# Feed-forward input as seven block products in place of eight, and the conditioning rows as matrix products in four column groups

## The chip, the cores and the metric

One core of one Trainium2 chip runs the whole program. The metric is the device time of one execution in microseconds (us). PE is the matrix engine, PEld its weight loads, DVE the vector engine, ACT the scalar engine, POOL the GpSimd engine, SP the engine whose queue issues the DMA transfers.

## The reference, cut to what matters

Two layers of a diffusion backbone on 640 tokens (128 of context, 512 latent), 1024 features. Each layer is a feed-forward half-step, a token mixing, and a second feed-forward half-step; each begins with an RMS norm and a modulation by rows computed from the condition:

```python
mods = (silu(cond) @ w_ada + b_ada).reshape(..., 9, 1, 1024)   # shift, scale, gate of three sub-layers
h = rmsnorm(x, g) * (1 + scale) + shift
x = x + 0.5 * gate * ((silu(h @ w_in[:, :2816]) * (h @ w_in[:, 2816:])) @ w_out)
```

`w_ada` is 1024 x 9216 for each layer, and there are two conditions, one for the context tokens and one for the latent ones. All is float32.

## The kernel before, in words

Features lie on the 128 partitions, tokens along the free dimension. The state `x` is eight tiles of 128 x 640. Matrix products run in the single-pass float32 type; to keep float32 accuracy each operand is split into a `hi` and a `lo` part, and each product is three passes: hi·hi, hi·lo, lo·hi (`mm3`; the matmul itself is recorded at line 128). For weights, ACT writes `hi` (line 156) and DVE `lo = raw - hi` (line 157) of 128 x 1024 elements at a time, two buffers of each. For activations the helper `split` does the same (lines 167 and 168).

A feed-forward (`ffn`) has 22 steps `pair(i)`: 128 gate columns and 128 up columns over eight contraction tiles, three passes and two halves of the tokens, 96 matmuls of 320 or 322 columns (two columns carry the shift). DVE takes each result out of PSUM and multiplies it by the norm's factor R (line 385), ACT applies SiLU (421), DVE multiplies (423), and `split` makes the operand of the output product. After 8, 15 and 22 pairs (`PARTS`) `out` runs the output product for each of eight tiles of `x`, and `x_update` (366) adds it with three DVE instructions. In the last part, and at the end of the token mixing (`mix`), `Norm.tile` prepares the next sub-layer's operand for each finished tile: squares on ACT (289), their running sum on POOL (291), the scaled `hi` on ACT (300) and `lo` on DVE (301), and the shift columns on POOL (309).

The conditioning rows: `ada_direct` computes three chunks of 512 columns at the start as float32 matmuls with the condition as the 128 x 2 stationary operand; the other 33 chunks are `ada_steps`, four blocks each, in which DVE multiplies a 128 x 1024 block of `w_ada` by the condition and sums it, once for each condition (244). A pump (`RATES`) spreads these blocks over the pairs and outputs of the feed-forwards.

The order of each engine's instructions is fixed when the program is built, by a list scheduler that takes the ready instruction that is earliest in the program by its own cost estimates. On the chip each engine runs its queue in that order, and an instruction waits for its semaphores with everything behind it. PSUM: two double-bank tiles (`PS`), two of one bank (`PH`), two of one bank (`PF`).

Of the kernel before, what the change touches and what calls it, by code (L numbers as in the profile page):

```python
# [25 lines left out]
RATES = (0.8, 0.8, 0.55)  # L26
# [10 lines left out]
PARTS = ((0, 8), (8, 15), (15, 22))  # L37
# [4 lines left out]
# the two halves of the tokens, without and with the columns of the shift  # L42
# [4 lines left out]
# columns of the per-partition vector table  # L47
# [14 lines left out]
class Pump:  # L62
    def __init__(self):
        self.q = []
# [11 lines left out]
def hybrid_step(ctx: ExitStack, tc: tile.TileContext, x_in, cc_in, cb_in, w_ada0, w_ada, pv_in, lam_in, w_fin, w_fout, w_min, w_mout,  # L76
                cache_in, ident_in, rope_in, cnt_in, sel_in,
# [6 lines left out]
    up = ctx.enter_context(tc.tile_pool(name="up", bufs=35))  # L84
# [19 lines left out]
    def E(dt=F32):  # L104
        return tp.tile([128, N], dt, tag="e", name=nm("e"), bufs=5)
# [33 lines left out]
    ident = C([128, 128], name="ident")  # L139
    sel = C([128, 2], name="sel")  # L140
    cnt = C([128, 2, 16], name="cnt")

    def load_raw(src, n):
        raw = wp.tile([128, 1024], F32, tag="raw", name=nm("raw"), bufs=3)
        nc.sync.dma_start(raw[:, :n], src)
        return raw

    def load_w(src, n, eng=None):
        """DRAM [128, n] -> (hi, lo) with hi + lo the weights exactly."""
        raw = load_raw(src, n)  # L150
        return split_w(raw, n, eng)

    def split_w(raw, n, eng=None):
        hi = wp.tile([128, 1024], F32R, tag="hi", name=nm("hi"), bufs=2)
        lo = wp.tile([128, 1024], F32R, tag="lo", name=nm("lo"), bufs=2)
        S.activation(hi[:, :n], raw[:, :n], AF.Copy)  # L156
        (eng or V).tensor_tensor(out=lo[:, :n], in0=raw[:, :n], in1=hi[:, :n], op=ALU.subtract)  # L157
        return hi, lo
# [13 lines left out]
    def lambdas():  # L172
        lv = T()
        nc.sync.dma_start(lv[:, :L * 128], lam_in)
        for l in range(L):
# [11 lines left out]
            lam.append(lm)  # holds -(lambda)  # L187
# [11 lines left out]
    def ada_direct(c, loads):  # L199
        """the products; yields before the row is turned into columns."""  # L200
# [15 lines left out]
    def ada_load(c, k):  # L216
        t = U(F32)
        nc.sync.dma_start(t[:, :512], w_ada0[:, k, c * 512:(c + 1) * 512])
        return t

    def silu_rows():
        """silu of the two conditions, along the free dimension of every partition."""
        r = []
        for i in range(2):
            t = up.tile([128, 1024], F32, tag="P", name=nm("sc"), bufs=3)
# [3 lines left out]
        return r  # L229

    def ada_steps(l, c, spare={}):
        m = []

        def step(b):
            if b == 0:
                m.append(C([128, 4, 2], name="mod"))
            if b in spare:
                raw = spare[b]
                nc.sync.dma_start(raw, w_ada[l, 4 * c + b])
            else:  # L240
                raw = load_raw(w_ada[l, 4 * c + b], 1024)
            dump = sp.tile([128, 1536], F32, tag="KS", name=nm("dump"), bufs=2)
            for i in range(2):
# [1091 lines left out]
```

## Time and profile before

| | |
|---|---|
| median of three runs | 2506.04 us (2505.41 to 2507.21) |
| span of the profiled execution | 2509.4 us |
| PE busy in it | 2446.1 us |
| DVE busy | 1563.7 us |
| ACT busy | 865.5 us |
| POOL busy | 304.9 us |

The profile gives the profiled execution's span and no separate time for it; the span is 3.4 us above the median of the runs. Busy times are sums of instruction durations; matmuls are pipelined, so the distance from one start to the next says more of PE than a duration.

### The profile page before, as it was taken

Reading aid. Unit: us, or ns where it says so; the run is one execution under the profiler, and the core shown is the slowest. Engines: PE = TensorE matmul, PEld = TensorE weight load, DVE = VectorE, ACT = ScalarE, POOL = GpSimd, SP = SyncE. Lnnn points to the kernel's source line nnn. Section 1 sums busy time; section 2 is a strip of 40 time slices with the busy share of each in tenths; the row PEclk is TensorE's granted clock in tenths of the full one; section 3 lists DMA queues with packets and bytes.
Section 4 is the critical chain, followed back from the end, with each engine's and each line's share of the span. In section 5 each row is a group of like instructions: output and inputs, shape, how many; then the busy total and the mean of one; then the engine's idle time right before and its main releaser. Section 6 shows DMA issues by size and latency. Waiting matters only on the chain. (4 is left out here: it accounts for less than half of the span.)

```text
span 2509.4 us, 39961 instructions
## 1 busy us (share of the span) xinstructions
PE 2446.1 (97%) x16529; PEld 2405.3 (96%) x16529; DVE 1563.7 (62%) x2550; ACT 865.5 (34%) x1417; POOL 304.9 (12%) x329
## 2 busy tenths in 40 slices
PE   8999999998998999999999999999999999999998
PEld 4999999998898999999999999999989999999998
DVE  5766766668886666666666556556788664334335
ACT  3222212356664221212332122224666442122223
POOL 3000000143224000000110000003513230000002
PEclk8999999999999999999999999999999999999999
DMA  7444444224322444444333333332242122222224
GB/s 261 154 142 136 132 138 138 90 89 137 117 66 89 137 135 135 133 137 135 101 110 110 120 115 116 115 102 89 90 143 85 53 74 70 75 76 70 82 72 130
DMA packets 91317, 282.10 MB, mean 112 GB/s; under 512 B 9600, under 2 KB 17664, under 8 KB 91136
## 3 DMA queue, kind: packets, MB, share of 16 engines
q1 hardware_dynamic: 91136, 279.56, 34.6%
q8 instruction: 130, 2.13, 0.3%
q14 instruction: 51, 0.42, 0.1%
HBM read 264.58 MB, written 14.94 MB: 111 GB/s over the span
## 5 line engine op out<-in xcount | busy, mean ns | idle before, releaser
L128 PE MATMUL S<-u,hi 128*128 128x320 f32 (+1 forms) x9056 | 1720.7, 311 | 14.8 <-DVE x L366 7.3
L128 PEld LDWEIGHTS S<-u,hi 128*128 128x128 f32 x9056 | 1434.7, 189 | 18.8 <-ACT hi L156 7.7
L128 PE MATMUL S<-u,lo 128*128 128x320 f32 (+2 forms) x4528 | 1047.6, 310 | 4.4 <-DVE lo L157 4.4
L128 PEld LDWEIGHTS S<-u,lo 128*128 128x128 f32 x4528 | 765.2, 189 | 5.4 <-DVE lo L157 5.4
L156 ACT ACTIVATE hi<-raw 128x1024 fp32r<-128x1024 f32 (+2 forms) x336 | 345.2, 1027 | 1117.7 <-PE S L128 649.9
L244 DVE SCALAR_TENSOR_TENSOR dump<-raw,sc 128x1024 f32<-128x1024 f32 x262 | 322.9, 1234 | 175.9 <-DMA raw<-in_w_ada_dram 172.7
L157 DVE TENSOR_TENSOR lo<-raw,hi 128x1024 fp32r<-128x1024 f32 (+1 forms) x296 | 351.3, 1187 | 10.7 <-ACT hi L156 8.0
L385 DVE TENSOR_TENSOR t<-S,R 128x642 f32<-128x642 f32 x176 | 145.2, 825 | 331.8 <-PE S L128 325.2
L128 PE MATMUL F<-u,hi 128*128 128x320 f32 (+1 forms) x1056 | 236.9, 316 | 3.9 <-DVE t L547 3.3
L366 DVE SCALAR_TENSOR_TENSOR x<-S,gate,x 128x128 f32<-128x128 f32 (+2 forms) x264 | 99.8, 433 | 184.8 <-PE S L128 184.6
L128 PEld LDWEIGHTS F<-u,hi 128*128 128x128 f32 x1056 | 175.1, 190 | 5.5 <-DVE t L547 3.8
L128 PE MATMUL F<-u,lo 128*128 128x320 f32 (+1 forms) x528 | 155.2, 313 | 0.0
L167 ACT ACTIVATE u<-t 128x640 fp32r<-128x640 f32 x88 | 65.1, 740 | 208.4 <-DVE t L423 208.4
L157 POOL TENSOR_TENSOR lo<-raw,hi 128x1024 fp32r<-128x1024 f32 (+1 forms) x40 | 89.4, 2234 | 258.3 <-ACT hi L156 212.2
L168 DVE TENSOR_TENSOR u<-t,u 128x640 fp32r<-128x640 f32 x88 | 72.6, 825 | 62.1 <-ACT u L167 62.1
L421 ACT ACTIVATE t<-t 128x128 f32<-128x128 f32 (+1 forms) x176 | 89.6, 556 | 57.2 <-DVE t L385 55.1
L301 DVE SCALAR_TENSOR_TENSOR u<-x,scl,u 128x128 fp32r<-128x128 f32 x96 | 94.3, 996 | 7.9 <-ACT u L300 6.9
L128 PEld LDWEIGHTS F<-u,lo 128*128 128x128 f32 x528 | 97.6, 190 | 0.0
L291 POOL TENSOR_TENSOR t<-t,t 128x640 f32<-128x640 f32 x42 | 73.5, 1749 | 161.6 <-ACT t L289 161.4
L568 POOL MEMSET pl<- 128x8 f32 x4 | 0.4, 107 | 761.2 <-DVE dump L244 761.1
L423 DVE SCALAR_TENSOR_TENSOR t<-t,t 128x128 f32<-128x128 f32 (+1 forms) x176 | 88.7, 545 | 0.0
L716 DVE TENSOR_REDUCE s<-S 128x1 f32<-128x640 f32 x96 | 77.4, 814 | 2.7 <-PE S L128 2.4
(184 smaller groups left out, 1382.6 us busy)
## 6 DMA issues: line engine op xcount, KB each, us to landing
raw<-in_w_fin_dram SPq DMA_DIRECT2D x176, 512.0 KB
raw<-in_w_ada_dram SPq DMA_DIRECT2D x131, 512.0 KB
raw<-in_w_fout_dram SPq DMA_DIRECT2D x72, 448.0 KB
raw<-in_w_min_dram SPq DMA_DIRECT2D x36, 512.0 KB
raw<-in_w_fout_dram SPq DMA_DIRECT2D x32, 512.0 KB
u<-in_w_ada_dram SPq DMA_DIRECT2D x24, 256.0 KB
KS<-kd SPq DMA_DIRECT2D x16, 384.0 KB
raw<-in_w_mout_dram SPq DMA_DIRECT2D x16, 384.0 KB
```

Of the source, the lines that this page charges most:

```text
L128: PE.matmul(out, lhsT, rhs, start=start, stop=stop)
L156: S.activation(hi[:, :n], raw[:, :n], AF.Copy)
L157: (eng or V).tensor_tensor(out=lo[:, :n], in0=raw[:, :n], in1=hi[:, :n], op=ALU.subtract)
L168: V.tensor_tensor(out=dst_lo, in0=src, in1=dst_hi, op=ALU.subtract)
L244: V.scalar_tensor_tensor(out=dump[:, :D], in0=raw, scalar=1.0, in1=rows[i], op0=ALU.mult, op1=ALU.mult, accum_out=m[0][:, b, i:i + 1])
L291: G.tensor_tensor(out=sq[:, :N], in0=sq[:, :N], in1=self.acc[:, :N], op=ALU.add)
L301: (eng or V).scalar_tensor_tensor(out=lo[:, a:b], in0=x[d][:, a:b], scalar=s, in1=hi[:, a:b], op0=ALU.mult, op1=ALU.subtract)
L366: V.scalar_tensor_tensor(out=xs, in0=ps[h][:, a:b], scalar=g[:, d % 4, c:c + 1], in1=xs, op0=ALU.mult, op1=ALU.add)
L385: V.tensor_tensor(out=t[:, :TX], in0=whole(ps), in1=norm.R, op=ALU.mult)
L421: S.activation(g[:, a:b], g[:, a:b], AF.Silu, bias=g[:, N + c:N + c + 1])
L423: V.scalar_tensor_tensor(out=u[:, a:b], in0=u[:, a:b], scalar=u[:, N + c:N + c + 1], in1=g[:, a:b], op0=ALU.add, op1=ALU.mult)
L716: V.tensor_reduce(out=m, in_=s[:, :, :HN], axis=AX.XY, op=ALU.max, negate=True)
```

## The change

`w_fin`'s pair is a 2 x 2 block matrix: gate and up columns by the first and the last four contraction tiles. The operand is a 2 x 2 block matrix as well: first and last four contraction tiles by two halves of the tokens. The changed `pair` forms their product with seven block products in place of eight, a Winograd form of Strassen's scheme: DVE adds blocks of weights (`s3`, `a21`, `s2`, `s4`), each of the seven weight blocks is split into hi and lo, and the seven products of 12 matmuls of 322 columns accumulate in two PSUM regions `A` and `D` that are read in between, and a third, `B`. The operand's seven forms are made by `FastNorm`, in place of `Norm`, once for each feed-forward: four sums on DVE and seven splits for each of four k. The first two pairs of the program stay plain (`NPLAIN`) while those forms are made. The parts of the output product are five in place of three, its tiles go in `ORDER`, and `x_update_joined` uses two DVE instructions in place of three. Weights are split 512 columns at a time, four buffers of each kind.

`ada_steps` goes: `ada_rounds` computes two chunks of 512 columns at a time in four steps. Each step loads two 128 x 1024 blocks of `w_ada` and issues four float32 matmuls, with a 128 x 32 stationary operand that holds the condition in two columns, each to its own 32 partitions of one PSUM bank. After the fourth step ACT copies the bank, and four small float32 matmuls with the 128 x 4 constant `groups` turn rows to columns and add the groups that belong together. A third buffer set (`P`) holds the blocks; `ada_direct` computes chunk 1 too. `E` tiles move to the pool of `U` tiles, 38 of them in place of 35.

```diff
-RATES = (0.8, 0.8, 0.55)
+RATES = (0.29, 0.29, 0.2)
-PARTS = ((0, 8), (8, 15), (15, 22))
+PARTS = ((0, 5), (5, 10), (10, 14), (14, 18), (18, 22))
...
+HLB = 4
+NPLAIN = 2
+ORDER = (0, 4, 1, 5, 2, 6, 3, 7)
+HW = N // 2 + 2
...
+    class Weights:
+
+
+        def __init__(self, raw, n, eng=None):
+            self.parts = [self.piece(raw[:, c:min(c + 512, n)], eng) for c in range(0, n, 512)]
+
+        @staticmethod
+        def piece(src, eng=None):
+            n = src.shape[-1]
+            hi = wp.tile([128, 512], F32R, tag="hi", name=nm("hi"), bufs=HLB)
+            lo = wp.tile([128, 512], F32R, tag="lo", name=nm("lo"), bufs=HLB)
+            S.activation(hi[:, :n], src, AF.Copy)
+            (eng or V).tensor_tensor(out=lo[:, :n], in0=src, in1=hi[:, :n], op=ALU.subtract)
+            return hi, lo
...
-    def silu_rows():
-            nc.sync.dma_start(t, cb_in[:, i * D:(i + 1) * D])
-            S.activation(t, t, AF.Silu)
-            r.append(t)
...
-    def ada_steps(l, c, spare={}):
...
-        def step(b):
...
-                raw = load_raw(w_ada[l, 4 * c + b], 1024)
-            dump = sp.tile([128, 1536], F32, tag="KS", name=nm("dump"), bufs=2)
-            for i in range(2):
-                V.scalar_tensor_tensor(out=dump[:, :D], in0=raw, scalar=1.0, in1=rows[i], op0=ALU.mult, op1=ALU.mult,
-                                       accum_out=m[0][:, b, i:i + 1])
-            if b == 3:
-                V.tensor_tensor(out=m[0], in0=m[0], in1=bada(l, c), op=ALU.add)
-                mods[l][c] = m[0]
...
+    def ada_rounds(l, c):
+
+
+        ps = []
+
+        def step(r):
+            if r == 0:
+                ps.append(PH())
+            for k in (2 * r, 2 * r + 1):
+                w = up.tile([128, 1024], F32, tag="P", name=nm("wa"), bufs=3)
+                nc.sync.dma_start(w, w_ada[l, k, :, c * 512:(c + 2) * 512])
+                for h in range(2):
+                    q = 32 * (2 * (k % 2) + h)
+                    PE.matmul(ps[0][q:q + 32, :], sc32[:, k, :], w[:, h * 512:(h + 1) * 512], start=r == 0, stop=r == 3)
+            if r == 3:
+                row = T()
+                S.activation(row[:, :512], ps[0], AF.Copy)
+                pt = PH()
+                for b in range(4):
+                    mm(pt[:, 4 * b:4 * b + 4], row[:, b * 128:(b + 1) * 128], groups, True, True)
+                for h in range(2):
+                    m = C([128, 4, 2], name="mod")
+                    V.tensor_tensor(out=m, in0=pt[:, 0:16].rearrange("p (b h c) -> p b h c", b=4, h=2)[:, :, h, :], in1=bada(l, c + h), op=ALU.add)
+                    mods[l][c + h] = m
+
+        return [lambda r=r: step(r) for r in range(4)]
...
+    class FastNorm:
...
+        def staged(self, d):
+            t = T()
...
+            for c, h, a, b in ((0, 0, 0, NC), (1, 0, NC, HN), (1, 1, HN, N)):
+                S.activation(t[:, a + 2 * h:b + 2 * h], x[d][:, a:b], AF.Copy, scale=self.scale(d, c))
+            G.tensor_copy(self.view(t)[:, :, HN:HW], self.shift_tile(d // 4)[:, d % 4])
+            return t
...
+        def sums(self, k, b1, b2, late=False):
+            B11, B12, B21, B22 = b1[:, :HW], b1[:, HW:], b2[:, :HW], b2[:, HW:]
+            n, m = T(), T()
+            N1, T3, N2, T4 = n[:, :HW], n[:, HW:], m[:, :HW], m[:, HW:]
+
+            def form(name, src):
+                u = self.view(U())
+                split(u[:, 0], u[:, 1], src)
+                self.f[name, k] = u
+
+            if not late:
+                form("B11", B11)
+                form("B21", B21)
+            V.tensor_tensor(out=T3, in0=B22, in1=B12, op=ALU.subtract)
+            V.scalar_tensor_tensor(out=N2, in0=T3, scalar=-1.0, in1=B11, op0=ALU.mult, op1=ALU.subtract)
+            form("N2", N2)
+            form("T3", T3)
+            V.tensor_tensor(out=N1, in0=B11, in1=B12, op=ALU.subtract)
+            form("N1", N1)
+            V.scalar_tensor_tensor(out=T4, in0=N2, scalar=-1.0, in1=B21, op0=ALU.mult, op1=ALU.subtract)
+            form("T4", T4)
+            if not late:
+                form("B22", B22)
...
+        def tile(self, d):
+
+            self.squares(d)
+            self.st[d] = self.staged(d)
+            if d >= 4:
+                self.sums(d - 4, self.st.pop(d - 4), self.st.pop(d))
...
+    def product(ps, piece, act, start):
+
+        hi, lo = piece
+        for k in range(4):
...
-        def pair(i):
...
+        def pair(i, first):
+
+
+            rg, ru = load_raw(wi[i, 0], 1024), load_raw(wi[i, 1], 1024)
+            a11, a12, a21, a22 = rg[:, :512], rg[:, 512:], ru[:, :512], ru[:, 512:]
+            s2, s3, s4 = FT([128, 512]), FT([128, 512]), FT([128, 512])
+            piece = Weights.piece
+
+            def add(o, a, b):
+                V.tensor_tensor(out=o, in0=a, in1=b, op=ALU.add)
+
+            p = PS()
+            A, D, B = p[:, 0, :HW], p[:, 1, :HW], PF()[:, :HW]
+            g, u = T(), T()
+            w = piece(a11)
+            product(A, w, norm.get("B11"), True)
+            S.activation(g[:, :HW], A, AF.Copy)
+            w = piece(a12)
+            add(s3, a11, a21)
+            add(a21, a21, a22)
+            add(s2, a21, a11)
+            product(B, w, norm.get("B21"), True)
+            if first:
+                norm.stats_sum()
+            V.tensor_tensor(out=g[:, :HW], in0=B, in1=g[:, :HW], op=ALU.add)
+            w = piece(s2)
+            product(A, w, norm.get("N2"), False)
+            S.activation(u[:, :HW], A, AF.Copy)
+            w = piece(s3)
+            add(s4, s2, a12)
+            product(D, w, norm.get("T3"), True)
+            S.activation(u[:, HW:], D, AF.Copy)
+            if first:
+                norm.stats_spread()
+            w = piece(a21)
+            product(A, w, norm.get("N1"), False)
+            V.tensor_tensor(out=u[:, HW:], in0=A, in1=u[:, HW:], op=ALU.add)
+            w = piece(a22)
+            product(D, w, norm.get("T4"), False)
+            V.tensor_tensor(out=u[:, :HW], in0=D, in1=u[:, :HW], op=ALU.add)
+            w = piece(s4)
+            product(A, w, norm.get("B22"), False)
+            V.tensor_tensor(out=g[:, HW:], in0=A, in1=norm.R[:, HW:], op=ALU.mult)
+            V.tensor_tensor(out=g[:, :HW], in0=g[:, :HW], in1=norm.R[:, :HW], op=ALU.mult)
+            V.tensor_tensor(out=u, in0=u, in1=norm.R, op=ALU.mult)
+            activation(i, g, u, HN)
...
-            hi, lo = load_w(wo[d, :, k0 * 128:k1 * 128], (k1 - k0) * 128)
-            mm3([ps[:, 0], ps[:, 1]], CN, hi, lo, acts[k0:k1], range(k1 - k0))
-            x_update(d, ps=[ps[:, 0], ps[:, 1]], gate=gate)
+            w = load_w(wo[d, :, k0 * 128:k1 * 128], (k1 - k0) * 128)
+            mm3(joined(ps), CN, w, acts[k0:k1], range(k1 - k0))
+            x_update_joined(d, ps, gate)
...
         gate = None
         for k0, k1 in PARTS:
             for i in range(k0, k1):
-                pair(i)
+                if l == 0 and sub == 0 and i < NPLAIN:
+                    plain_pair(i)
+                    if i == 0:
+                        for k in range(4):
+                            norm.late(k)
+                else:
+                    pair(i, i == 0)
+            while gate is None and mods[l][2 * (3 * sub + 2) + 1] is None:
+                pump.step()
...
-                for d in range(KT):
+                for d in ORDER:
                     out(k0, k1, d, gate, nx)
         return nx
...
```

## Rows read from the trace of the kernel before

**Rows 1.** The page's first part: busy us, share of the span, instructions.
```profile
PE 2446.1 (97%) x16529; PEld 2405.3 (96%) x16529; DVE 1563.7 (62%) x2550; ACT 865.5 (34%) x1417; POOL 304.9 (12%) x329
```

**Rows 2.** Stages: window, length, busy of PE, PEld, DVE, ACT, POOL; clock, DMA, GB/s.
```profile
200.00:494.00 294.00, 294.00 (x2000) 294.00 (x2000) 191.00 (x296) 75.95 (x101) 9.88 (x18) 1.00 0.40 128
2040.00:2440.00 400.00, 400.00 (x2717) 400.00 (x2715) 156.55 (x210) 98.21 (x124) 0.00 (x0) 1.00 0.23 74
```

**Rows 3.** Whom PE waited for, longest first: us, times, longest.
```profile
PE S L731 <- ACT e L722: 14.8, 12, 2.7
PE S L128 <- DVE x L366: 7.3, 6, 1.7
```

**Rows 4.** Timeline of DVE over one pair: start, us, what.
```profile
1310.65 0.82 DVE L385 TENSOR_TENSOR t<-S,R 128x642 f32<-128x642 f32 x1
1311.39 1.21 DVE L157 TENSOR_TENSOR lo<-raw,hi 128x1024 fp32r<-128x1024 f32 x1
...
1324.92 0.82 DVE L385 TENSOR_TENSOR t<-S,R 128x642 f32<-128x642 f32 x1
```

**Rows 5.** Groups of instructions with shapes apart: busy us, mean ns, idle before.
```profile
L244 DVE SCALAR_TENSOR_TENSOR dump<-raw,sc 128x1024 f32<-128x1024 f32 x262 | 322.9, 1234 | 175.9 <-DMA raw<-in_w_ada_dram 172.7
L157 DVE TENSOR_TENSOR lo<-raw,hi 128x1024 fp32r<-128x1024 f32 x224 | 273.1, 1219 | 9.8 <-ACT hi L156 8.0
L168 DVE TENSOR_TENSOR p<-S,p 128x512 fp32r<-128x512 f32 x64 | 43.8, 685 | 8.8 <-ACT p L167 8.4
L547 DVE TENSOR_TENSOR t<-F,R 128x322 f32<-128x322 f32 x24 | 11.7, 488 | 9.4 <-PE F L128 9.3
L168 DVE TENSOR_TENSOR u<-t,u 128x640 fp32r<-128x640 f32 x88 | 72.6, 825 | 62.1 <-ACT u L167 62.1
L423 DVE SCALAR_TENSOR_TENSOR t<-t,t 128x512 f32<-128x512 f32 x88 | 65.6, 745 | 0.0
L167 ACT ACTIVATE p<-S 128x512 fp32r<-128x512 f32 x64 | 38.2, 597 | 26.9 <-DVE p L168 17.0 <-PE H L128 4.8 <-PE S L731 4.2
L421 ACT ACTIVATE t<-t 128x512 f32<-128x512 f32 x88 | 62.4, 709 | 0.0
```

**Rows 6.** Timeline of PE at the start: float32 matmuls, then the first shift.
```profile
37.41 7.03 PE L128 MATMUL F<-u,silu_c 128*2 128x512 f32 x16
45.18 0.41 PE L211 MATMUL H<-ident,t 2*128 2x2 f32 x4 [0.74 <-ACT t L207]
45.52 1.28 PE L128 MATMUL H<-ones,t 128*128 128x1 f32 x10
...
50.60 0.64 PE L128 MATMUL S<-u,hi 128*128 128x322 f32 x1 [3.02 <-POOL u L309]
```

**Rows 7.** Timeline of PE in an output product.
```profile
160.27 0.45 PE L128 MATMUL S<-u,lo 128*128 128x320 f32 x2
160.56 0.75 PE L128 MATMUL S<-u,hi 128*128 128x320 f32 x4
161.15 0.45 PE L128 MATMUL S<-u,lo 128*128 128x320 f32 x2
```

**Rows 8.** Timeline of DVE at the end of a token mixing.
```profile
785.10 1.12 DVE L366 SCALAR_TENSOR_TENSOR x<-S,mod,x 128x128 f32<-128x128 f32 x3
786.15 1.26 DVE L301 SCALAR_TENSOR_TENSOR u<-x,scl,u 128x512 fp32r<-128x512 f32 x2
787.33 0.66 DVE L366 SCALAR_TENSOR_TENSOR x<-S,mod,x 128x128 f32<-128x128 f32 x2
787.91 1.59 DVE L301 SCALAR_TENSOR_TENSOR u<-x,scl,u 128x512 fp32r<-128x512 f32 x1
789.43 0.54 DVE L366 SCALAR_TENSOR_TENSOR x<-S,mod,x 128x320 f32<-128x320 f32 x1
789.89 0.33 DVE L301 SCALAR_TENSOR_TENSOR u<-x,scl,u 128x128 fp32r<-128x128 f32 x1
790.15 1.12 DVE L366 SCALAR_TENSOR_TENSOR x<-S,mod,x 128x128 f32<-128x128 f32 x3
```

More of the change, by code (lines that the diff above doesn't have):

```diff
@@ L380, in tick, with activation @@
                 credit[0] -= 1.0
-        def pair(i):
-            def evac(ps):
+        def activation(i, g, u, cb):
+            lb = HW + HN
+            for a, b, c in ((0, NC, cb), (NC, lb, lb)):
+                S.activation(g[:, a:b], g[:, a:b], AF.Silu, bias=g[:, c:c + 1])
+            for a, b, c in ((0, NC, cb), (NC, lb, lb)):
+                V.scalar_tensor_tensor(out=u[:, a:b], in0=u[:, a:b], scalar=u[:, c:c + 1], in1=g[:, a:b],
+                                       op0=ALU.add, op1=ALU.mult)
+            hi, lo = U(), U()
+            split(*[t[:, :N].rearrange("p (h n) -> p h n", h=2) for t in (hi, lo)], FastNorm.view(u)[:, :, :HN])
+            acts[i] = (hi, lo)
+            tick(2.0)
@@ L384, in evac, with plain_pair, half @@
+        def plain_pair(i):
+            def half(ps, w, h):
+                n = (HN, HW)[h]
+                for k in range(KT):
+                    w0, w1 = w.at(k)
+                    a = norm.f[norm.blocks(k)[h], k % 4]
+                    ah, al = a[:, 0, :n], a[:, 1, :n]
+                    for p, (w_, a_) in enumerate(((w0, ah), (w0, al), (w1, ah))):
+                        mm(ps[:, :n], w_, a_, k == 0 and p == 0, k == KT - 1 and p == 2)
+            def evac(p, sign):
                 t = T()
-                V.tensor_tensor(out=t[:, :TX], in0=whole(ps), in1=norm.R, op=ALU.mult)
@@ L386, in evac @@
-                return t
-            first = w_first if l == 0 and sub == 0 and i == 0 else None
-            hi, lo = first[0] if first else load_w(wi[i, 0], 1024)
-            p = PS()
-            pg = halves(p)
-            if first:
-                hi2, lo2 = first[1]
-                p2 = PS()
-                pu = halves(p2)
-                mm3(pg, CX, hi, lo, norm.xp, hs=(0,))
-                mm3(pu, CX, hi2, lo2, norm.xp, hs=(0,))
+                for h, n in enumerate((HN, HW)):
+                    V.scalar_tensor_tensor(out=t[:, h * HW:h * HW + n], in0=p[:, h, :n], scalar=sign, in1=norm.R[:, h * HW:h * HW + n],
+                                           op0=ALU.mult, op1=ALU.mult)
@@ L797, in mix @@
         rq8 = [None, None]
-        kxs = [sp.tile([128, 2, 128], F32R, tag="kc", name=nm("kx"), bufs=3) for _ in range(2)]
+        kxs = [FT([128, 2, 128], F32R, "kx") for _ in range(2)]
         gvcx = vctx_tiles()
@@ L1139, in mix @@
         ends = mix_ends()
-        for d in range(KT):
+        for i, d in enumerate(ORDER):
             if d in opened:
@@ L1187, in hybrid_step @@
     lds[0] = [ada_load(0, k) for k in range(KT)]
-    rows = silu_rows()
-    for f in ada_steps(0, 1, {3: cache_tile()}):
-        f()
-    c0 = ada_direct(0, lds[0])
+    lds[1] = [ada_load(1, k) for k in range(KT)]
+    c0, c1 = ada_direct(0, lds[0]), ada_direct(1, lds[1])
     def first_shift():
         next(c0), next(c0), next(c0, None)
+        next(c1), next(c1), next(c1, None)
         for d in SHO:
@@ L1199, in hybrid_step @@
     nc.sync.dma_start(cnt, cnt_in)
+    nc.sync.dma_start(groups, groups_in)
     pump = Pump()
@@ L1247, in _tables @@
     sel[64:, 1] = 1.0
-    return dict(ident=np.eye(128, dtype=np.float32), rope=rope, cnt=cnt, sel=sel)
+    groups = np.zeros((128, 4), np.float32)
+    for q in range(4):
+        for c in range(2):
+            groups[32 * q + c, 2 * (q % 2) + c] = 1.0
+    return dict(ident=np.eye(128, dtype=np.float32), rope=rope, cnt=cnt, sel=sel, groups=groups)
 def _layout(i):
```

243 lines of the change are left out of this document (150 added, 93 removed).

## The prediction

> **What bounds the kernel now.** I read the shares of the whole page first: PE is busy 97% of the span, DVE 62% [rows 1]. Shares are averages, so I then took stages. In two long stretches of feed-forward PE is busy for every microsecond, with the clock at its upper level, while DVE is free for 35% and 61% of the time [rows 2]. The list of whom PE waited for says the same: its longest entries, 14.8 us for the softmax of the token mixing and 7.3 us for the state update, are small beside 2509.4 us [rows 3]. So a feed-forward costs what PE's matmuls cost, and the reader should expect the change to be decided by PE's sum: what leaves PE against what comes to it.
>
> One pair is 14.27 us from one evacuation to the same one of the next pair [rows 4]; over 96 matmuls that is 0.1486 us each. In the output product six matmuls of 320 columns take 0.88 us from start to start, 0.147 us each [rows 7].
>
> **What leaves PE.** 86 of the 88 pairs go from 96 matmuls to 84: 86 x 12 x 0.1486 = 153.4 us. Such a pair is then 84 x 0.1486 = 12.5 us. The token mixing and the output products keep their matmuls.
>
> **What comes to PE.** The conditioning blocks leave DVE: 262 instructions, 322.9 us [rows 5]. DVE bounded nothing in those stages, so their absence gives back nothing by itself. They come back as 16 calls of `ada_rounds`, 64 steps of four float32 matmuls with 512 columns. The nearest row is `ada_direct`, whose eight matmuls of 512 columns appear as 16 instructions in 7.03 us, so each float32 matmul is two instructions of 0.44 us [rows 6]. The stationary operand there has 2 columns and here 32, and all outputs there begin at partition 0. No row shows matmuls in different column groups side by side. The bounds for a step are therefore eight instructions in a row, 3.52 us, and four groups side by side, 2 x 0.44 = 0.88 us; for 64 steps 225 us and 56 us. I take a value between: the two instructions of a matmul stand next to each other in the queue and need the same columns. If PE starts instructions in queue order, the second of group 0 waits for the first, and the first of group 1 can start only beside it. Each following group adds one slot: five slots for four groups, 2.2 us, and 64 x 2.2 = 141 us.
>
> By the Trainium skill, page "TensorE: Matmul & The Clock Gate", section "Part 3: Packing small matmuls", matmuls on different tiles overlap but begin and end strictly in program order; no run here shows it yet. By that rule the sum is the one I take.
>
> The turn of rows to columns: 16 calls x 4 float32 matmuls, two instructions each, by the ten of the norm's sum in 1.28 us [rows 6]: 128 x 0.128 = 16 us. At the start `ada_direct` for chunk 1 adds 16 x 0.44 + 0.4 = 7.4 us, of which the 3.0 us that PE waited for the shift's copies can be covered [rows 6]; I take 4, bounds 0 and 7.4.
>
> **What DVE gets.** Per pair: seven `lo` and four sums of 512 columns (0.685 us), five instructions of 322 columns (0.488), one of 644 and one `lo` of 640 (0.825 each), two multiplications (1.09 together) [rows 5]. Sum of durations: 7.5 + 2.4 + 1.65 + 1.1 = 12.7 us. Neighbours in the queue overlap by 0.08 us (a 0.82 us instruction is followed after 0.74) [rows 4]; for 20 instructions that leaves 11.1 us. PE has 12.5. So DVE is at 90% or just over the top, and the cost lies between nothing and, with 12.7 plus 0.5 us of waiting for ACT's halves, 0.7 us a pair, 60 us in all. Buffers for four pieces let splits run three products ahead, 5.4 us, against 0.6 + 0.69 us to make one, so I take 0.2 us a pair: 17 us. If that cover goes, PE stands behind each `lo` for about 1.3 us, in program order with everything queued. ACT gets seven halves (0.597) and three copies (about 0.45): with the SiLU (two, about 1.1) and the split (0.74) some 7.4 us a pair, under PE's time [rows 5].
>
> **Where stages meet.** `FastNorm` makes seven splits and four sums for two tiles of the state, 11 instructions of 322 columns: 5.5 x 0.41 to 0.49 = 2.3 to 2.7 us of DVE a tile. Now two tiles take 5.05 us at the end of the mixing, 2.3 of it state update, so 1.4 us a tile is the present preparation [rows 8]. New time a tile: 2.5 - 1.4 + 2.5 = 3.6, where PE's twelve matmuls take 1.8. That is 9 us over eight tiles, at the ends of two mixings. In the last part of the middle feed-forward, PE has 24 x 0.147 = 3.5 us a tile and DVE 1.0 + 0.6 + 2.5 = 4.1: 5 us. With a microsecond each for the last forms, 26 us, bounds 10 and 40. The first forms of the program are hidden behind the two plain pairs (28.5 us).
>
> Five parts in place of three put the chain from the last product through SiLU to the split, some 6 us, at eight more places; what hides it is the other PSUM tile's output product, up to 2 x 3 x 0.88 = 5.3 us for parts of four pairs. I take 5 us, bounds 0 and 20. Against these gaps, the conditioning matmuls depend on nothing near them and can fill some: -8 us of the 22. Their loads are as many as before but no longer share the weights' buffers; DVE waited 172.7 us for them in 131 blocks [rows 5], and PE would stand 1.3 us a load if three buffers were not enough, but they are asked for a step ahead, which is over 20 us at the pump's new rate. That `E` moves to the pool of `U` I cost at nothing: 38 tiles in place of 40 hold what a mixing has open; 10 us if they don't.
>
> **The sum**, on the profiled span: 2509.4 - 153.4 + 141 + 16 + 4 + 17 + 26 + 5 - 8 = 2557. The median of the runs is 3.4 below the span: 2553.6, slower by 1.9%.
>
> **The rivals.**
>
> *All four groups side by side* (faster). Then a step is 0.88 us, 85 us less in all: 2469 us. For it: the matmuls of a step are independent, write different partitions, and stand together. Against it: the order of the pairs of instructions above. It decides from a step of 1.46 us on: without the 141 us the sum is 2416, and (2509.4 - 2416) / 64 = 1.46. The Trainium skill, page "TensorEngine Tiling (Array Packing)", section "Theoretical Speedup", gives up to four times for dimensions of at most 32; by it the time would be this rival's. No row here bears it out or excludes it.
>
> *No overlap at all* (slower still). A step is 3.52 us: 84 us more, 2638. For it: every float32 matmul of the trace follows the one before by its full 0.44 us [rows 6], though all of those are in the same columns.
>
> *DVE as the bound of the pairs.* Durations as they stand make 12.7 us against PE's 12.5, and an order fixed by estimates leaves holes on an engine that is nearly full. At 0.9 us lost a pair in place of 0.2 it gives 60 us more: 2614.
>
> **How the numbers follow.** Chances: five slots a step 0.40; side by side 0.32; no overlap 0.18; DVE as the bound 0.10. The likeliest gives 2554, its own range 2525 to 2590 by the bounds of the small terms. The range over the cases reaches from 2452, below the side-by-side case with its small terms at their lower ends, to 2628; left out are most of the no-overlap case above it (about 0.12) and 0.05 below. What a measurement of this kernel can tell from no change is about 0.2%, 5 us. Faster: the side-by-side case and a little of the likeliest with its terms low, 0.33. Same: 0.06, where a step comes near 1.46 us. Slower: 0.61.
>
> **What would show it.** In the changed profile: a pair of 84 matmuls should be 12.5 to 12.9 us long; a step of eight float32 instructions should start over about 1.8 us and end after 2.2, each group's first instruction beside the second of the group before. Starts a few nanoseconds apart and 0.9 us in all would mean the first rival; 0.44 us between all of them the second. DVE over 95% busy in the pairs, with PE waiting for `lo`, would mean the third. At the end of the mixings the waits of PE for the state update should grow from 7 to about 25 us. The prediction is wrong above all if a step costs under 1.46 us, or if pairs take 13 us or more.

## The result, and the profile after

The changed kernel takes 2733.95 us (median of 4 runs, 2733.24 to 2738.06) against 2506.62 for the kernel before: ratio 1.091, 95% interval 1.0895 to 1.0926. I had forecast 2554, at most 2628. The direction came out as forecast, the size did not: 180 us are missing in my sum. The direction was luck: with the 89 us that the conditioning is measured at below, in place of my 149, my own sum would have said 2494, faster.

The page of the changed kernel, its line of busy times (they count overlapping instructions once, so they are not sums of durations; the line of before is in [rows 1]):

```profile
PE 2542.1 (93%) x16157; PEld 2320.0 (85%) x16157; DVE 1843.4 (67%) x3450; ACT 1231.4 (45%) x2460; POOL 301.0 (11%) x375
```

PE has 372 instructions fewer, and its share of the span went down, not up: it stands. The list of whom PE waited for (total us, times, longest) names the place; the entries of before are in [rows 3]:

```profile
PE S L497 <- ACT t L620: 45.5, 49, 1.2
PE S L497 <- ACT hi L169: 21.0, 34, 0.6
PE S L134 <- DVE x L511: 18.0, 6, 4.5
PE H L134 <- DMA u<-qd: 11.2, 3, 8.5
...
PE H L258 <- DMA wa<-in_w_ada_dram: 4.6, 8, 1.4
```

The two longest entries are matmuls of `product` (L497) that waited for ACT, for the copy of the sum A (L620) and for the `hi` of a piece (L169). Together they are 66.5 us, less than the 158 that they turn out to cost: the list counts from the recorded end of the matmul before, and it leaves out 35 of the 86 pairs, where conditioning matmuls stand where the other 49 have the first of the two waits. A pair in the last feed-forward, where no conditioning runs, from one multiplication by R to the next on DVE (start, duration; before [rows 4]):

```profile
2353.14 0.82 DVE L637 TENSOR_TENSOR t<-t,R 128x644 f32<-128x644 f32 x1
...
2368.07 0.82 DVE L637 TENSOR_TENSOR t<-t,R 128x644 f32<-128x644 f32 x1
```

So 14.93 us, where I had 12.5 to 12.9 and the kernel before 14.27. Within that pair PE's timeline (start, duration; in brackets the idle time and what ended it) shows where it stands:

```profile
2357.82 0.31 PE L497 MATMUL S<-u,lo 128*128 128x322 f32 x1
2359.09 0.57 PE L497 MATMUL S<-u,hi 128*128 128x322 f32 x2 [0.96 <-ACT t L620]
...
2360.83 0.31 PE L497 MATMUL S<-u,lo 128*128 128x322 f32 x1
2361.77 0.90 PE L497 MATMUL S<-u,hi 128*128 128x322 f32 x4 [0.62 <-ACT hi L169]
```

From start to start these two places take 1.27 and 0.94 us where neighbours take 0.15: 1.12 and 0.79 us lost, and five of 0.1 beside them; the matmuls themselves are as fast as before. ACT at the same time:

```profile
2358.08 0.63 ACT L169 ACTIVATE hi<-f 128x512 fp32r<-128x512 f32 x1 [0.20 <-PE S L497]
2358.61 0.42 ACT L620 ACTIVATE t<-S 128x322 f32<-128x322 f32 x1
...
2361.09 0.63 ACT L169 ACTIVATE hi<-raw 128x512 fp32r<-128x512 f32 x1 [0.81 <-PE S L497]
2361.62 0.42 ACT L624 ACTIVATE t<-S 128x322 f32<-128x322 f32 x1
```

Read the rows together. Products are named by their operand's form (N2, T3 and so on). The last matmul of N2 that reads its `hi` ends at 2357.98, and N2, into A, at 2358.13. ACT makes a `hi` that had waited for the buffer which N2 held, then copies A, and at 2359.09, with the copy done, the product T3 begins. But T3 writes D, the other bank. In the built program its first matmul waits for just the count that the copy L620 reaches; N1, into A, waits for the copy of D (L624); T4, into D, for DVE's reading of A (L629); and B22, into A, for DVE's reading of D (L632). Each waits for one reading more than its own bank needs. A and D are `p[:, 0]` and `p[:, 1]` of one tile.

The second place is less direct. The matmuls at 2361.77 and 2362.02 are not N1's: they belong to the next pair's first product and stand ahead of N1 in PE's queue. They wait for their `hi`, which had waited for the buffer that T3 held. N1 begins behind them at 2362.17, just after the copy of D has ended (2362.04).

The conditioning is another matter than I thought. A step whose eight instructions stand together, and a split one (six):

```profile
74.54 1.07 PE L258 MATMUL H<-wa,sc 128*32 128x512 f32 x8
75.54 0.42 PE L497 MATMUL F<-u,hi 128*128 128x322 f32 x1
...
133.58 1.06 PE L258 MATMUL H<-wa,sc 128*32 128x512 f32 x6
```

The groups do run side by side: in the trace the first instructions of the four matmuls start 7 ns apart and the second ones, again 7 ns apart, 0.45 us later. But only 22 steps stand together; most are split into three matmuls and one, and each piece costs about 1 us. Counted from the starts of PE's instructions around each insertion, the 64 steps take 119 us, 1.86 each.

### The profile page after: what moved, and what is told of

It reads as the page before. It is cut to its first block, busy times and chain, and to the rows that moved or that the text cites. A ratio compares the mean times of both kernels' runs of the same rounds, so it can differ in the third digit from the quotient of the medians.

```text
span 2731.3 us, 42282 instructions
## 1 busy us (share of the span) xinstructions
PE 2542.1 (93%) x16157; PEld 2320.0 (85%) x16157; DVE 1843.4 (67%) x3450; ACT 1231.4 (45%) x2460; POOL 301.0 (11%) x375
## 5 line engine op out<-in xcount | busy, mean ns | idle before, releaser
L497 PE MATMUL S<-u,hi 128*128 128x322 f32 x4128 | 964.6, 322 | 70.7 <-ACT t L620 45.5
L497 PEld LDWEIGHTS S<-u,hi 128*128 128x128 f32 x4128 | 685.3, 189 | 193.9 <-ACT t L620 89.1
L169 ACT ACTIVATE hi<-raw 128x512 fp32r<-128x512 f32 (+2 forms) x696 | 414.1, 596 | 868.9 <-PE S L497 384.5
L134 PE MATMUL S<-u,hi 128*128 128x320 f32 (+3 forms) x3552 | 698.4, 315 | 35.9 <-DVE x L511 18.0
L497 PE MATMUL S<-u,lo 128*128 128x322 f32 x2064 | 629.2, 310 | 0.0
L134 PEld LDWEIGHTS S<-u,hi 128*128 128x128 f32 x3552 | 567.7, 191 | 61.4 <-ACT hi L169 18.6
L170 DVE TENSOR_TENSOR lo<-raw,hi 128x512 fp32r<-128x512 f32 x616 | 398.9, 649 | 181.4 <-ACT hi L169 173.9
L134 PE MATMUL S<-u,lo 128*128 128x320 f32 (+3 forms) x1776 | 421.2, 312 | 2.6 <-DVE lo L170 2.6
L497 PEld LDWEIGHTS S<-u,lo 128*128 128x128 f32 x2064 | 392.1, 191 | 0.8 <-issue 0.8
L169 ACT ACTIVATE hi<-f 128x512 fp32r<-128x512 f32 x258 | 162.3, 631 | 250.9 <-PE S L497 174.0
L170 DVE TENSOR_TENSOR lo<-f,hi 128x512 fp32r<-128x512 f32 x258 | 177.3, 687 | 38.6 <-ACT hi L169 33.0
L497 PE MATMUL F<-u,hi 128*128 128x322 f32 x688 | 157.4, 314 | 0.9 <-ACT hi L169 0.7
L629 DVE TENSOR_TENSOR t<-S,t 128x322 f32<-128x322 f32 x86 | 42.4, 493 | 154.3 <-PE S L497 154.3
```

Source lines behind the costliest of these rows:

```text
L134: PE.matmul(out, lhsT, rhs, start=start, stop=stop)
L169: S.activation(hi[:, :n], src, AF.Copy)
L170: (eng or V).tensor_tensor(out=lo[:, :n], in0=src, in1=hi[:, :n], op=ALU.subtract)
L497: PE.matmul(ps, w_, a, start=start and k == 0 and p == 0, stop=k == 3 and p == 2, skip_group_check=True)
L629: V.tensor_tensor(out=u[:, HW:], in0=A, in1=u[:, HW:], op=ALU.add)
```

## Experiments

**Theories.** *One tile*: a product waits for the evacuation of the product before it, since the two sums share a tile; remove that, and the pair is 12.5 to 13 us. *Ring*: the four buffers of `hi` and `lo` are too few, and PE stands behind pieces ("if that cover goes", in my prediction). DVE as the bound, my third rival, falls by the rows already: it is busy for 298.41 of 441 us in the last feed-forward (the row stands under e1).

**e1, A and D in tiles of their own.**

```diff
-            p = PS()
-            A, D, B = p[:, 0, :HW], p[:, 1, :HW], PF()[:, :HW]
+            A, B, D = PS()[:, 0, :HW], PF()[:, :HW], PF()[:, :HW]
```

> Edit: the sums A and D of a pair, two banks of one PSUM tile in the changed kernel, get a tile each (D takes the second buffer of the F pool); nothing else. One-tile theory: a product into one bank waits for the evacuation of the other, because both are one tile. In the changed kernel's steady pair (14.93 us) the matmuls alone take 84 x 0.149 = 12.5; the two long stalls are 1.12 and 0.79 us. Without the waits a pair should be 12.5 to 13.0 us, so 86 x 2.0 to 2.4 = 170 to 210 us go; in the order of the instructions 53 of the conditioning steps now stand with all four matmuls together, against 22, about 1 us less each, another 20 to 35. Together 2490 to 2545 us. Ring theory: PE waits because the four buffers of hi and lo let a piece be made only when the product four before it is done; the ring is unchanged here, so pairs stay above 14 us and the time above 2650.

2575.53 us, 158 less. The pair of e1 on DVE, and then the last feed-forward in windows of after (first row) and of e1 (second): busy us of PE, PEld, DVE, ACT, POOL with their counts, granted clock, DMA.

```profile
2344.92 0.82 DVE L636 TENSOR_TENSOR t<-t,R 128x644 f32<-128x644 f32 x1
...
2357.56 0.82 DVE L636 TENSOR_TENSOR t<-t,R 128x644 f32<-128x644 f32 x1
```

```profile
2244.00:2685.00 441.00, 407.57 (x2619) 387.88 (x2617) 298.41 (x527) 175.21 (x319) 0.00 (x0) 1.00 0.22 71
```

```profile
2135.00:2530.00 395.00, 394.69 (x2644) 391.76 (x2643) 303.03 (x537) 176.52 (x324) 0.00 (x0) 1.00 0.25 81
```

The pair is 12.64 us here, 12.62 in most, and PE idles for 0.3 of 395 us. The one-tile theory stands. The time is 30 us above the range I gave it, so the rest lies outside the pairs. e1 changes more than the waits: the scheduler now puts 53 steps together in place of 22, and counted as above the 64 steps take 87 us in place of 119. In the last feed-forward, which has no steps, e1 gains 49 us; in the first three 36, 32 and 42.

**e2 and e3, a fifth buffer of hi and lo**, with A and D in one tile (e2) and in two (e3).

```diff
-HLB = 4
+HLB = 5
...
-        t = up.tile([128, 1024], F32R, tag="P", name=nm("p"), bufs=3)
+        t = up.tile([128, 1024], F32R, tag="P", name=nm("p"), bufs=2)
```

> Edit: on the changed kernel, five buffers of hi and lo in place of four (paid for with two in place of three of the tiles of 1024 columns that the conditioning loads and the mixing share); A and D stay one tile. One-tile theory: the waits for the evacuations stay, but a copy no longer stands behind a hi that waits for a buffer (0.63 us): the stall behind N2 goes from 1.12 to about 0.5, the one behind T3 from 0.79 to about 0.4, so 1.0 us a pair and 86 us in all: about 2645, 2600 to 2690. Ring theory: nearly all of the 2.4 us a pair goes: 2520 to 2560.

> Both edits: A and D in tiles of their own, and five buffers of hi and lo. One-tile theory: no more than 20 us under the run with the tiles of their own alone, or the same. If the ring is a second, independent stall of a pair, another 0.3 to 0.6 us a pair go, 25 to 50 us.

e2: 2701.62, e3: 2589.05. In e2 the steady pair falls by the 1.0 us expected (most are 13.9 us; the last feed-forward 423 us in place of 442), but the buffers given up cost 14 and 9.5 us in the mixings, and the total misses my range by 12 us. In e3 the pair is the same 12.6 us as in e1; the time is 13.5 us longer, 7 and 11 of it in the mixings. The ring delays the copy that PE waits for; once PE no longer waits for that copy, it costs the pairs nothing.

**e4, all conditioning matmuls in one column group** (on e1; both chunks of a call are now summed into one row, so the modulation is another one).

```diff
-                    q = 32 * (2 * (k % 2) + h)
-                    PE.matmul(ps[0][q:q + 32, :], ...
+                    PE.matmul(ps[0][0:32, :], ...
...
```

> Edit: on the kernel with A and D in tiles of their own, all conditioning matmuls write the first column group, so that both chunks of a call are summed into one row and the modulation is another one; the number of matmuls and their shapes stay. In the changed kernel a step whose eight instructions stand together takes 1.08 us of PE's queue (first instructions 7 ns apart, the second ones 0.45 us later). Theory of overlapping groups: in one group each of the eight takes about 0.45 us by itself, a step 3.5 us, so 64 x 2.4 = 155 us more than with four groups. Rival, that the instructions would overlap in one group as well: the same time within 10 us.

2727.8 in its one run, 152 more than e1. The step there:

```profile
76.64 3.62 PE L257 MATMUL H<-wa,sc 128*32 128x512 f32 x8
```

3.62 us against 1.07: the four groups are what makes them overlap. For 64 steps that would be 163 us.

**e5, all pairs as eight products**, the rest as changed.

```diff
-                if l == 0 and sub == 0 and i < NPLAIN:
-                    plain_pair(i)
...
-                else:
-                    pair(i, i == 0)
+                plain_pair(i, i == 0)
```

> Edit: the changed kernel with all 88 pairs as eight products (the kernel's own plain pair), and with the operands that these need; five parts, buffers and conditioning matmuls stay. It prices everything of the change but the seven products. With tiles of their own the seven products' pair is 12.62 us against 14.27, so 142 us are given back here. Terms as measured there: 2509 before, 87 to 119 for the conditioning matmuls, 15 for the turn of rows, and the rest of what the run with own tiles lost (about 100 us in all between its 2573 and 2509 - 142 + 87 + 15), less what the sums of the FastNorm cost at the stages' ends (my 26): 2640 to 2700. If the seven products were what loses that rest, this run would be at 2610 to 2640 instead.

2671.36: without any of the seven products the change costs 165 us. Against it e1, with the seven products and tiles of their own, is 96 us shorter. The next two runs take the 165 apart on the kernel before.

**e6, only the shared pool; e7, only the five parts.**

```diff
-        return tp.tile([128, N], dt, tag="e", name=nm("e"), bufs=5)
+        return up.tile([128, UW], dt, tag="U", name=nm("e"))
```

```diff
-PARTS = ((0, 8), (8, 15), (15, 22))
+PARTS = ((0, 5), (5, 10), (10, 14), (14, 18), (18, 22))
```

> Edit: the kernel before, with the softmax's tiles e taken from the pool of the tiles u (38 in all) in place of five of their own beside 35. In the kernel with own tiles the two token mixings, from the last SiLU of one feed-forward to the first of the next, are 369 and 367 us against 360 and 356, though three pairs' output products (21 us) fewer lie in them, so they lose some 31 and 34 us; matmuls of the attention stand there with 20 us more between them in the first. Theory that the shared pool does it: 15 to 20 us a mixing, 2535 to 2550. My forecast's price for the move was nothing, or 10 us.

> Edit: the kernel before, with five parts of the feed-forward in place of three, nothing else. My forecast: 5 us, bounds 0 and 20. From the last feed-forward of the run with own tiles, 436 us against 467 with 36 to be expected from its 22 pairs, 5.5 us a feed-forward, so 22 us in all: 2510 to 2530.

e6: 2560.58, 54 us more, nearly all of it in the two mixings (22 and 25); e7: 2537.35, 31 us more. Both above what I expected. The first mixing in windows, before (first) and e6 (second), and the longest wait of PE in e6's:

```profile
458.30:818.10 359.80, 336.84 (x2319) 327.22 (x2318) 268.09 (x498) 202.67 (x408) 122.59 (x120) 0.99 0.30 98
```

```profile
459.40:841.40 382.00, 347.68 (x2325) 336.23 (x2324) 264.64 (x498) 201.56 (x408) 121.48 (x120) 0.96 0.27 92
...
PE H L128 <- DMA u<-qd: 9.9, 2, 8.6
```

The same matmuls, 11 us more idle time, and a granted clock of 0.96 in place of 0.99 (means over the stretch; 1.00 is the upper of its two levels). The wait is for the transfer of a head's queries into a `u` tile, which came late.

In e7 no single wait stands out, but the stages of the table below tell where its time lies. Three pairs' output products, 144 matmuls or 21 us, move into each feed-forward from the stage behind it. Less these, the first feed-forward is 8 us longer, the second and the last 1 each and the third 2; the stretch between the second and the third is 8 longer, the end 6 and the second mixing 3. So the eight new places cost hardly anything in three of four feed-forwards, and in the last one PE never stands:

```profile
2065.20:2486.60 421.40, 421.40 (x2856) 420.54 (x2855) 178.87 (x275) 102.96 (x138) 0.00 (x0) 1.00 0.22 73
```

More than half of the loss, 17 us, lies where the last part's output product has to cover the preparation of the next stage, and that part is now four pairs in place of seven. That the shorter cover is the cause is my reading; no run changes the last part alone.

**e8, the conditioning on DVE again** (on e1; `ada_steps` of the kernel before in place of `ada_rounds`; the blocks are loaded into the third tile of the set `P`, whose other two hold the condition).

> Edit: the kernel with own tiles, with the conditioning back on DVE (the rows' products with the accumulated sum, two of 1.23 us a block, 128 blocks, loads into the third of the conditioning's buffers). It takes 87 us of matmuls and 15 us of the turn off PE and puts 316 us on DVE, which is busy for 11.1 of the 12.6 us of a pair. Theory that the output products leave DVE enough room: 2573 - 100 = 2470 to 2490. Rival, that DVE bounds the pairs then: of the three feed-forwards with conditioning each has 105 us more on DVE and PE waits for lo: at half of it hidden, 2573 - 100 + 160 = 2630.

2552.82, 23 us less and not 100. Windows of e8's first and second feed-forward:

```profile
62.00:500.00 438.00, 412.08 (x2671) 403.06 (x2670) 406.27 (x758) 184.00 (x362) 10.20 (x15) 0.98 0.40 127
881.00:1294.00 413.00, 399.54 (x2628) 393.49 (x2627) 385.14 (x712) 170.77 (x323) 1.40 (x7) 0.99 0.41 129
```

DVE is busy for 93% of both, and in the first PE stands for 26 us of the 438. With seven products the rows' products no longer lie beside PE for nothing: against e1 the second and third feed-forward gain 15 and 17 us, the first loses 2. My third rival is true of this kernel's first feed-forward, not of the changed kernel. A part of the miss has another place, the first mixing, which is 12 us longer than e1's; its cause stays open.

**e9, 33 tiles u and five e, not shared** (kernel before), and **e10, e in tiles of its own** (on e1; T4's forms go into two tiles that only the mixing uses; 34 tiles u in place of 38, and four e).

```diff
-    up = ctx.enter_context(tc.tile_pool(name="up", bufs=35))
+    up = ctx.enter_context(tc.tile_pool(name="up", bufs=33))
```

```diff
+                if name == "T4":
+                    if k % 2 == 0:
+                        self.ks = sp.tile([128, 1536], F32R, tag="KS", name=nm("k4"), bufs=2)
+                    u = self.view(self.ks[:, k % 2 * UW:(k % 2 + 1) * UW])
...
-        return up.tile([128, UW], dt, tag="U", name=nm("e"))
+        return tp.tile([128, N], dt, tag="e", name=nm("e"), bufs=4)
```

> Edit: the kernel before with 33 tiles u and five tiles e of their own: as many tiles in all as in the run with the shared pool (38 in place of 40), but not shared. That run lost 54 us, 22 and 25 of it in the two mixings. Theory that sharing does it (a short-lived e takes the next buffer in turn, and so waits for long-lived tiles and they for it): 2506 to 2515. Rival, that the number of tiles does it: 2545 to 2560.

> Edit: the kernel with A and D in tiles of their own; the forms T4 go into the two tiles of 1536 columns that only the mixing uses otherwise, the pool of u goes from 38 to 34 and e gets four tiles of its own. Theory of the shared pool: what it cost in the kernel before (54 us) comes back, less what one e tile and one u tile fewer cost: 2520 to 2540. Rival, that the mixings of that kernel lose their time to something else of the change (weights in pieces of 512 with four buffers): above 2560.

e9: 2520.04, so 14 us come from two tiles fewer and 40 from sharing. e10: 2523.62, 52 us under e1; its mixings take 342 and 345 us where e1's take 369 and 367.

**e15, own e with A and D still one tile** (the changed kernel with e10's edit).

> Edit: the changed kernel with A and D still the two banks of one tile, and only the e tiles and forms moved as in the run with own e. If the two causes, the false wait in the pairs and the shared pool in the mixings, are independent, it comes to 2734 - 52 = 2682, 2672 to 2692, and the two mixings shorten by 22 to 27 us each. If one hides a part of the other, it stays above 2692.

2688.73, 45 us less than the changed kernel, where the same edit took 52 from e1: the two causes are nearly independent.

**e14, no conditioning** (on e11, below; the modulation is the bias alone).

> Edit: on the run with the steps together, the sixteen calls of ada_rounds leave out their loads, matmuls and turn of rows: the modulation is the bias alone. It prices the conditioning on PE by itself. Worked out from the trace of that run, by starts of PE's instructions around each insertion: 83 us for the steps and 14.5 for the turns, so 2521 - 98 = 2423, 2415 to 2432. If these matmuls fill gaps that PE has anyway (my forecast's 8 us, and more in the changed kernel as it was), it is above 2432; if their loads and the waits behind them cost more than their own time, below 2415.

2432.47: the conditioning on PE costs 89 us where its steps stand together, 9 less than its instructions take (83 for the steps, 14.5 for the turn of rows). The 9 are gaps that it fills. One shows in e14, behind the two plain pairs, whose time was to hide the first forms: PE waits there 3.7 us for one of them, and from 75 to 90 us it idles for 4.8 us at a granted clock of 0.77. In e10, with conditioning steps there, the same stretch has 0.3 us of idle time and a clock of 1.00.

**e11 to e13 and e16, towards a faster kernel.** e11 issues both loads of a step ahead of its matmuls; e12 puts the conditioning of the second and third feed-forward on DVE, with its elementwise output in the three tiles F that hold the sums of weights; e13 gives that output a tile of its own (paid for with 20 small tiles in place of 32); e16 puts it into the tile of the caches.

In order, the cores of e11, e12 and e16:

```diff
+            ws = []
             for k in (2 * r, 2 * r + 1):
...
+                ws.append((k, w))
+            for k, w in ws[::-1]:
```

```diff
-            pump.add(ada_rounds(l, c))
+            pump.add(ada_steps(l, c) + ada_steps(l, c + 1) if dve else ada_rounds(l, c))
```

```diff
-                V.scalar_tensor_tensor(out=FT([128, 512]).bitcast(mybir.dt.bfloat16), in0=w, ...
+                V.scalar_tensor_tensor(out=cache_tile(), in0=w, ...
```

> Edit: on the one with own e, both loads of a conditioning step are issued before its matmuls, which go the second load first. In the order of instructions 58 steps of 64 then stand with their four matmuls together, against 53, and six are split, where there were 11 in two to four pieces. A split costs 1 us each: 8 to 12 us less than the run with own e, 2510 to 2530.

> Edit: on the one with the steps together, the conditioning of the second and third feed-forward is on DVE (the first keeps its matmuls). With all of it on DVE these two stages were 15 and 17 us shorter and what lies between them and behind them 5, while the first gained nothing and the mixing behind it lost 12. Theory: 30 to 38 us less than with the steps together, 2475 to 2500, below the kernel before. Rival, that the rows' products now compete with the pairs for the three small tiles of the sums (they take their output's place): no gain, 2510 to 2550.

> Edit: on the hybrid, the rows' products write their elementwise output to a tile of its own (1024 columns of bfloat16) in place of the ring of three tiles that holds the sums of the pairs. In the hybrid the second feed-forward took 437 us from its first SiLU to its last, in the run with all conditioning on DVE and a free output tile 413; the third took 395 in both. Theory that the shared ring makes the difference: 2509 - 24 = 2485, 2478 to 2500, under the kernel before. Rival, that the rate of the blocks on DVE does it: 2500 to 2512.

> Edit: as in the run with an output tile of its own, but the rows' products write to the tile that holds the mixing's caches, whose load for the second layer moves to just before its mixing; the small tiles are 32 again in place of 20. In the run before, the second feed-forward took 412 us as expected, but the first mixing 354 where the runs with 32 small tiles took 342. Theory that the small tiles did that: 11 us less, 2492, 2485 to 2499. Rival, that the first mixing's loss has another cause, or that the moved load is late at the second mixing: 2500 to 2510.

e11: 2521.32, 2 us less, within noise of e10, and not 8 to 12: the 64 steps, counted as above, took 86 us in e10 and take 83 here. e12: 2509.03, outside both of its ranges; of the feed-forwards only the third gained. In the second PE waits for pieces whose sums wait for a tile F (first row, e12; second, e13):

```profile
PE S L531 <- ACT hi L169: 22.7, 15, 4.5
```

```profile
PE S L531 <- ACT hi L169: 6.9, 3, 2.4
```

e13: 2503.18, ratio 0.9985 (0.9976 to 0.9994); e16: 2502.62, ratio 0.9987 (0.9978 to 0.9996). The second feed-forward came to 412 us as expected, but the mixing ahead of it is 10 us longer than in e10 to e12, in e16 too: it was not the small tiles, and what it was stays open. So both times lie in their rivals' ranges, though the second feed-forward went as the theories had it. The best version is a hair under the kernel before, 0.13%, which is less than the 0.2% that I took as no change.

Stage lengths in us, from the ends of the SiLU instructions in each trace (a feed-forward from its first pair's to its last pair's; between them the last output products and the mixing):

| stage | before | after | e1 | e5 | e6 | e7 | e10 | e16 |
|---|---|---|---|---|---|---|---|---|
| feed-forward 1 | 397.5 | 471.9 | 435.7 | 457.7 | 399.4 | 426.8 | 433.4 | 436.1 |
| mixing 1 | 359.8 | 367.9 | 369.4 | 369.2 | 382.0 | 339.3 | 342.4 | 352.4 |
| feed-forward 2 | 399.8 | 459.9 | 428.3 | 455.1 | 401.2 | 421.8 | 428.6 | 412.2 |
| between 2 and 3 | 68.9 | 64.2 | 63.8 | 54.7 | 68.4 | 55.7 | 63.6 | 60.8 |
| feed-forward 3 | 400.2 | 454.1 | 412.6 | 441.1 | 400.0 | 423.4 | 412.7 | 402.6 |
| mixing 2 | 355.7 | 369.6 | 367.3 | 364.6 | 381.2 | 337.7 | 344.5 | 340.3 |
| feed-forward 4 | 399.4 | 441.6 | 392.7 | 419.7 | 400.2 | 421.4 | 392.5 | 392.2 |
| end | 67.3 | 42.9 | 43.2 | 50.0 | 67.6 | 52.1 | 43.0 | 43.1 |

With five parts the last part has four pairs in place of seven, so some 21 us of output products move from "mixing", "between" and "end" into the feed-forward ahead of them; compare sums there. In a pair of seven products SiLU also stands later: in e5 it ends 5 us before the last pair's last product, in e1 1.5 us behind it, and the end is 6.8 us shorter. So these two are compared by their whole times.

## Why the prediction was wrong, point by point

**What leaves PE** was right as a sum of matmuls. My 14.27 us was one pair [rows 4]; in the last feed-forward of the kernel before, a pair is 14.17:

```profile
2369.33 0.83 DVE L385 TENSOR_TENSOR t<-S,R 128x642 f32<-128x642 f32 x1 [2.46 <-PE S L128]
...
2383.50 0.83 DVE L385 TENSOR_TENSOR t<-S,R 128x642 f32<-128x642 f32 x1 [2.46 <-PE S L128]
```

The clean pair of e1, 12.62, is 1.55 us under it: 133 us over 86 pairs, where 153.4 less 17 for losses was forecast. **The step that failed is the loss of a pair.** I bounded it by DVE and by the pieces, "between nothing and ... 0.7 us a pair", and took 0.2. That is what is left in e1 (84 matmuls at 14.17 / 96 make 12.40), but in the changed kernel it is 2.4 us, and neither DVE nor the pieces by themselves make it: a product waits for the evacuation of a sum in another bank, because both are one tile. I asked when the pieces that a product reads are ready, and never what the tile that it writes is still read by. e1 prices it at 158 us, by itself enough for a slower kernel, split steps included. Both signs that I had named for a wrong forecast came: a step under 1.46 us where it stands together, and pairs over 13. The stages with conditioning gain less from e1 than the last one does, since conditioning matmuls stood in a part of the stalls, at 35 of the 86 pairs.

**E in the pool of u**, which "I cost at nothing" on the count of tiles, is the second failed step: 52 us by e10, 45 by e15, 54 by e6. The count alone makes 14 (e9); sharing makes the rest.

**Five parts**: 5 forecast, bounds 0 and 20; 31 measured (e7). The place was wrong as well: I priced the chain at eight new places, and by e7's stages more than half of the loss lies in the stretches that the last part's output product has to cover.

**What comes to PE**: 141 + 16 - 8 = 149 forecast, 89 measured where the steps stand together (e14). The mechanism of my likeliest case, five slots a step, is wrong; the first rival's is right, 1.07 us a whole step near its 0.88, and the second rival's 3.52 is what one group takes (3.62 in e4). In the changed kernel a step still came to 1.86 us, between the two, since most were issued in two pieces. By the Trainium skill, "TensorEngine Tiling (Array Packing)", section "Theoretical Speedup", the factor is at most four for a dimension of at most 32; the trace gives 3.62 / 1.07 = 3.4. The Trainium skill's rule of program order ("TensorE: Matmul & The Clock Gate", "Part 3: Packing small matmuls") does not hold as I applied it, to the two instructions of one float32 matmul: here the second of the first group starts after the first of all four. So the first rival had the right mechanism and not the time: without the 158 us this kernel would still be slower than before, 2575.53.

**Where stages meet**: 26 forecast, bounds 10 and 40. Of the 133 us of matmuls, 96 arrive between e5 and e1, so the seven products lose some 37 outside the steady pairs. That is all that they bring there, not the ends of stages alone: about 11 of it are steps, which take 76 us in e5 and 87 in e1. The stretch between the second and the third feed-forward, e5 and e1:

```profile
1342.80:1397.50 54.70, 51.52 (x348) 49.18 (x347) 36.13 (x64) 26.09 (x55) 18.68 (x30) 1.00 0.29 97
```

```profile
1293.50:1357.30 63.80, 52.10 (x311) 49.38 (x310) 48.10 (x96) 37.80 (x87) 19.36 (x16) 0.87 0.20 67
```

It is 9 us longer, for which I had 6. But DVE, by whose sum I had reckoned it, is busy for 48 of 64 us; PE stands for 12 in place of 3, in single waits of up to 3.4 us, and the granted clock is 0.87 in place of 1.00. The waits of PE for the state update at the mixings' ends went from 7.3 [rows 3] to 18.0, not to 25. **The start**: 4 forecast; the first SiLU ends at 59.3 us against 60.9.

The sum with the measured terms: 2507 - 133 + 158 + 52 + 31 + 89 + 37 = 2741, 7 over the 2734. The terms come from different kernels: 52, 31 and 89 make 172, and e5, which has all three at once, costs 165.

## What to carry to other kernels

A chain that accumulates in turns in two banks needs two tiles: for each product, list who still reads the tile that it writes, not only the bank. A cost put at nothing on a count ("38 tiles in place of 40") needs an experiment of its own: who holds the tiles, and in which order they come free, was worth three times the count. Work saved on the engine that bounds a kernel can be paid back in the buffers that it takes: here 133 us of matmuls stand against 52 of shared tiles, 31 of shorter parts and 37 lost around the pairs, before any wait inside them.

## What was not expected of the hardware

Four float32 matmuls with 32 stationary columns in four column groups took 1.07 us for 512 columns, against 3.62 us in one group, and a run of three groups took 1.06, hardly less. The granted clock in the first mixing fell from 0.99 to 0.96 when waits were added (e6), and 11 us more idle time became 22 of length: the busy time of before, 336.84 us, times 0.99 / 0.96 is 347.4, and e6's is 347.68.
